# A streaming encoder step on one core: the last phase takes subln_g into A's weights, moves two transposes and the cached upper halves, and shortens a root

## The chip, the core and the metric

The kernel runs on one core of a Trainium2 chip. The metric is the time of one execution on the device in microseconds (us). Five engines work side by side, each through its own instructions in a fixed order: TensorE (PE in the profile; its weight loads are PEld), VectorE (DVE), ScalarE (ACT), GpSimd (POOL) and SyncE (SP), which here issues all transfers between the memories. SBUF and PSUM are the on-chip memories of 128 partitions; matrix products land in PSUM, in banks of 512 float32 per partition.

## What is computed

One layer for 2048 frames of a new stream (16 tiles of 128 rows) and for 8 running streams with 16 new frames each (one more tile of 128 rows, "the sample tile", with caches of 512 past keys and values for each stream). Two attention branches, A (four heads of 128 values, a difference of two softmaxes) and B (eight heads, stick-breaking), end in a merge:

```python
oa = rms_norm(oa, subln_g) * (1.0 - lam_init)
ya = (oa.reshape(b, s, WIDTH_A) * jax.nn.silu(za)) @ w_branch_a
yb = (ob.reshape(b, s, WIDTH_B) * jax.nn.silu(zb)) @ w_branch_b
return (jax.nn.sigmoid(ga) * ya + jax.nn.sigmoid(gb) * yb) @ w_out
```

The result, times a gate, is added to x, and a last rms_norm with final_g gives y. subln_g has 128 values, the same for each head of A.

## The kernel before

Every product that must be exact is made of float16 halves: `split` writes an upper half `hi = f16(src * s)` with a power of two `s`, and VectorE the lower half `lo = src * s - hi`; a product is then three float16 products (hi hi, hi lo, lo hi). The upper half is made by ScalarE, by GpSimd or by VectorE, by the last argument of `split` (lines 266 to 274). `scales` finds `s` from a sum of squares, six tiny VectorE instructions with the reduction; `rsqrt` finds a root from a guess by bits and three Newton steps, 15 instructions on VectorE for one column (lines 227 to 244).

First come the projections and the attention of the 16 prompt tiles, with o, z (the inputs of silu) and g (ga and gb) parked in DRAM. The last phase, which is what nearly all of the change touches, takes one tile after the other:

- `inputs(t)` (from line 1113) loads o, z and g, multiplies A's half of o with the root of its squares and with g8 (subln_g times 0.8, line 1127: one instruction for each head), makes silu (sigmoid of z on ScalarE into a PSUM bank of the tag "mm", o * z on GpSimd at 1132, times the sigmoid on VectorE at 1133), the sigmoids of g, then u16, the float16 halves of u, and turns them over to uT with 16 transposes on TensorE (`transposed`, 1106 to 1111, into banks of the tag "s", copied by ScalarE).
- `branches(st)` makes four products of 12 matmuls (1235, two columns halves of 512 for A and for B, banks "mm"), scales each by iu and g on VectorE (1237) and adds A and B on GpSimd (1239). After the last, `finish` cuts y into y16 and turns it to yT.
- `output(t, st)` makes two products of 24 matmuls with w_out (1274), the gate (1278), the sum with x on GpSimd (1282), the root of its squares, the last scaling (1287) and the store (1288).

There are two banks "mm" (branches and sigmoids), three "s" (transposes and the sample's scores), two "o" and one "t". Of o2, z2, u16, y16 and yT there is one buffer each, of uT two, of g2 four (two tiles).

Round n of the loop emits the branches of tile n, `inputs` of tile n + 2 and the output of tile n - 1; the first two `inputs` run before, during the end of the attention, with the cuts of the branch weights (`early_work`). Beside it run the pieces of the sample lane (`sample`, in the first 13 rounds): for each of 8 units, four loads of cached keys and four of cached values (512 KB each), each cut into halves (lines 715 and 751; the upper half on GpSimd), the keys turned over by a transposing DMA (717), the scores, the weights and 96 to 192 small matmuls (766).

The order in which the text emits work is a priority and not the final order. The framework plans the program on a simulated timeline

```python
with tile.TileContext(nc, schedule_with_timeline_sim=True) as tc:
```

and gives each engine, SP's queue among them, a fixed order: whatever the plan held to be ready, the earliest emitted first. On the chip an instruction waits for its inputs, and all behind it on its engine wait too.

Of the kernel before, what the change touches and what calls it, by code (L numbers as in the profile page):

```python
# [16 lines left out]
F32 = mybir.dt.float32  # L17
# [94 lines left out]
def layer_kernel(ctx: ExitStack, tc: tile.TileContext, a: dict):  # L112
# [132 lines left out]

    def sum_squares(src, n, dst, width=1024):

        for i in range(0, n, width):
            junk = tiny.tile([P, width], F16, tag="junk", name="junk", bufs=1)
            w = min(width, n - i)  # L250
            S.activation(out=junk[:, 0:w], in_=src[:, i : i + w], func=AF.Square,  # L251
                         accum_out=dst[:, i // width : i // width + 1])
# [26 lines left out]
    nlam = con.tile([P, 1], F32, name="nlam")  # L279
    g8 = con.tile([P, P], F32, name="g8")  # L280

# [403 lines left out]
    def sample(U, dec, qpad, cs):  # L685
# [115 lines left out]
    def norms():  # L801

        srcs = [w[:, k, :] for w in (w_ba, w_bb) for k in range(4)] + [w_out[:, k, :] for k in range(KT)]
        srcs = [(src, wsums[:, i : i + 1]) for i, src in enumerate(srcs)]
        srcs += [(caches[name][:, i * 8 : i * 8 + 8, h * P : (h + 1) * P], csums[:, cache_column(name, h), i : i + 1])
                 for name in caches for h in range(4) for i in range(4)]

        def one(src, dst):
            st = wst.tile([P, 2, 4, P], F32, tag="wst", name="wst").rearrange("p k j n -> p (k j n)")
            load(out=st if len(src.shape) == 2 else st.rearrange("p (j n) -> p j n", n=P), in_=src)  # L810
            sum_squares(st, 1024, dst)

        return [lambda src=src, dst=dst: one(src, dst) for src, dst in srcs]

# [60 lines left out]
    with tc.tile_pool(name="p0", bufs=1) as p0:  # L875
# [223 lines left out]
    def cut(dst, src, k, j, s, n, pool, tag, bufs):  # L1099

        st = pool.tile([P, 2, 512], F32, tag=tag, name="wst2", bufs=bufs)
        cols = slice(j * 512, (j + 1) * 512)
        load(out=st, in_=src[:, k : k + 2, cols])
        split(dst[:, 0, k : k + 2, cols], dst[:, 1, k : k + 2, cols], st, s[:, 0:1], S if n % 2 else G)

# [7 lines left out]
    def inputs(t):  # L1113
# [10 lines left out]
        r = L["orms"][:, 4 * t : 4 * t + 4] if t < NT else rsqrt(osums[:, NT, :], 4, P, tiny, "rA")  # L1124
        for h in range(4):
            c = slice(h * P, (h + 1) * P)
            V.scalar_tensor_tensor(out=o[:, c], in0=o[:, c], scalar=r[:, h : h + 1], in1=g8, op0=ALU.mult, op1=ALU.mult)  # L1127
        for n in range(2):
            c = slice(n * 512, (n + 1) * 512)
            sg = bank("mm")  # L1130
            act(out=sg, in_=z[:, c], func=AF.Sigmoid)
            G.tensor_tensor(out=o[:, c], in0=o[:, c], in1=z[:, c], op=ALU.mult)
            V.tensor_tensor(out=o[:, c], in0=o[:, c], in1=sg, op=ALU.mult)  # L1133
        for g in gs:
# [11 lines left out]
        return dict(u=uT, iu=iu, g=gs)  # L1146

# [4 lines left out]
    def early_work():  # L1152
# [13 lines left out]
        made = [lambda k=k, j=j, br=br: cut(L["wb"][:, br, :, :, :], (w_ba, w_bb)[br], k, j, L["s"][0], br + k, stage, "wst2", 1)  # L1166
                for br in range(2) for k in (0, 2) for j in range(2)]
# [35 lines left out]
    with ExitStack() as c2:  # L1203
# [9 lines left out]
        for n, (k, j) in enumerate((k, j) for j in range(2) for k in range(0, KT, 2)):  # L1213
            cut(wo, w_out, k, j, s_o, n, s2, "x", 2)
        gate = res.tile([P, D], F32, name="gate")
# [10 lines left out]
        def branches(st):  # L1226
# [16 lines left out]
            def finish():  # L1243
# [8 lines left out]
                yT = s2.tile([P, 16, P], F16, tag="yT", name="yT", bufs=1)  # L1252
                for half in range(2):
                    transposed(y16, yT, half)
                iy = unit.tile([P, 1], F32, tag="iy", name="iy")
                V.tensor_tensor(out=iy, in0=sy[:, 1:2], in1=s_o[:, 1:2], op=ALU.mult)
                st["y"], st["iy"] = yT, iy

            return [(2.6, lambda j=j, br=br: half(j, br)) for j in range(2) for br in range(2)]

        def output(t, st):
            box = {}

            def half(j):
# [18 lines left out]
                if j == 1:  # L1283
                    acc = tiny.tile([P, 1], F32, tag="facc", name="facc")
                    sum_squares(x, D, acc)
                    r = rsqrt(acc, 1, D, tiny, "rF")
                    V.scalar_tensor_tensor(out=x, in0=x, scalar=r, in1=fg, op0=ALU.mult, op1=ALU.mult)
# [60 lines left out]
```

## Time and profile before

| | us |
|---|---|
| median of 3 runs | 2494.43 (2491.0 to 2498.75) |
| the profiled execution | 2503.67 |
| its span, first to last instruction | 2501.9 |

| engine | busy us | share of the span |
|---|---|---|
| TensorE | 2162.8 | 86% |
| VectorE | 1807.2 | 72% |
| ScalarE | 1602.2 | 64% |
| GpSimd | 833.8 | 33% |

The first matmul of a branch product starts at 1922.8 us. The sample lane's last cut lies at 2365 us, the last output matmul ends near 2489 us, and the span ends at 2501.9 us. A busy share is a mean over stages with different limits, so the prediction reads the last phase in stretches. Where rows of waits are shown, an engine stood idle before the instruction on the left until the one on the right had ended.

### The profile page before, as it was taken

The numbers are of one execution on the slowest core, as the hardware profiler recorded it, in microseconds if no ns is written. First come the engines' busy times: TensorE is split into PE (matmuls) and PEld (weight loads), VectorE is DVE, ScalarE is ACT, GpSimd is POOL, SyncE is SP. The second block draws the span as 40 slices with busy tenths as digits, with TensorE's granted clock in tenths as the row PEclk, the third lists the DMA queues.
The fourth block names the chain that finished last, engine by engine and source line by source line (L and its number), as shares of the span: only waits on it lengthen the run. The fifth ranks groups of instructions, "written<-read, shape, count | busy, mean of one in ns | idle before, by whom it ended". The sixth has DMA issues, their size and how long they took to land.

```text
span 2501.9 us, 45310 instructions
## 1 busy us (share of the span) xinstructions
PE 2162.8 (86%) x16366; PEld 1263.7 (51%) x16366; DVE 1807.2 (72%) x3769; ACT 1602.2 (64%) x3200; POOL 833.8 (33%) x671
## 2 busy tenths in 40 slices
PE   4779898889989988899989889999975789888887
PEld 2445465545655555556555555555543344444443
DVE  4868657876665788667668866656787888787855
ACT  4658667876766778666677866656775545454442
POOL 1822023352101335321124532102353465443422
PEclk7989999999999999999999999999986889899999
DMA  8779778996777899777688976656678998997521
GB/s 304 270 184 215 183 185 202 207 209 158 187 204 170 202 206 223 169 158 184 165 201 190 217 178 168 168 134 141 146 170 214 270 232 238 225 237 209 155 97 52
DMA packets 890994, 477.07 MB, mean 191 GB/s; under 512 B 540074, under 2 KB 842330, under 8 KB 890256
## 3 DMA queue, kind: packets, MB, share of 16 engines
q1 hardware_dynamic: 890768, 474.17, 76.2%
q8 instruction: 128, 2.10, 0.4%
q14 instruction: 98, 0.80, 0.1%
HBM read 272.94 MB, written 73.44 MB: 138 GB/s over the span
## 4 chain that ended last, share of the span: by engine, by line
PE 40%; DMA 19%; DVE 16%; ACT 9%; issue 8%; POOL 4%; SPq 3%; DVEq 0%; POOLq 0%; ACTq 0%
PE ps_mm L409 16%; PE ps_t L476 9%; DMA hg<-hT_d 5%; DMA wt<-sc_n 4%; DMA wst<-in_w_in_dram 3%; DVE sc_n L588 3%; PE ps_s L611 2%; PE ps_mm L1235 2%; PE ps_s L612 2%; ACT junk L251 2%; ACT sc_p L121 2%; PE ps_o L1274 2%; DVE sc_n L545 1%; ACT ps_s L121 1%; DVE o L1127 1%
## 5 line engine op out<-in xcount | busy, mean ns | idle before, releaser
L409 PE MATMUL ps_mm<-wpair,hg 128*128 128x512 f16 x3120 | 790.1, 388 | 58.5 <-DMA hg<-hT_d 54.8
L594 POOL TENSOR_TENSOR sc_p<-sc_p,sc_n 128x127 f32<-128x127 f32 (+7 forms) x192 | 313.5, 1637 | 808.5 <-DVE sc_n L588 790.8
L409 PEld LDWEIGHTS <-hg 128*128 128x128 f16 x3120 | 279.2, 99 | 330.7 <-DMA hg<-hT_d 67.2
L476 PE MATMUL ps_t<-gw,hg 128*128 128x256 f16 (+1 forms) x2856 | 393.8, 292 | 2.5 <-DVE qst L504 1.7
L476 PEld LDWEIGHTS <-hg 128*128 128x128 f16 x2856 | 278.7, 99 | 96.3 <-DVE qst L504 2.5
L588 DVE TENSOR_TENSOR_SCAN sc_n<-ps_s,sc_n,zero_t 128x512 f32<-128x512 f32 x192 | 245.6, 1279 | 69.2 <-ACT ps_s L121 64.5
L611 PE MATMUL ps_s<-k,qst 128*128 128x512 f16 (+3 forms) x640 | 228.1, 358 | 52.4 <-DVE sc_n L588 41.3
L545 DVE TENSOR_TENSOR sc_n<-sc_p,sc_n 128x128 f16<-128x128 f32 (+7 forms) x192 | 234.5, 1227 | 36.8 <-ACT sc_n L544 36.2
L121 ACT ACTIVATE sc_p<-ps_s,usc 128x512 f32<-128x512 f32 (+3 forms) x320 | 204.8, 640 | 48.7 <-PE ps_s L612 24.0
L612 PE MATMUL ps_s<-k,qst 128*128 128x512 f16 (+3 forms) x640 | 227.6, 358 | 0.0
L1235 PE MATMUL ps_mm<-wb,uT 128*128 128x512 f16 x816 | 200.0, 398 | 21.4 <-DVE o L1133 13.0
L121 ACT ACTIVATE ps_s<-ps_s,usc 128x512 f32<-128x512 f32 (+3 forms) x328 | 199.8, 609 | 0.0
L1274 PE MATMUL ps_o<-wo,yT 128*128 128x512 f16 x816 | 193.8, 392 | 6.7 <-POOL wo L271 4.8
L663 PE MATMUL ps_o<-v,wt 128*128 128x128 f16 x1088 | 162.3, 228 | 42.4 <-DMA wt<-sc_n 42.4
L544 ACT CAST sc_n<-sc_p 128x128 f16<-128x128 f32 (+7 forms) x192 | 154.8, 813 | 44.3 <-POOL sc_p L594 43.4
L442 POOL TENSOR_TENSOR rot<-pr,rope 128x256 f32<-128x256 f32 x68 | 60.5, 890 | 358.7 <-ACT pr L423 314.6
L251 ACT ACTIVATE junk<-wst 128x1024 f16<-128x1024 f32 x124 | 131.4, 1059 | 71.8 <-DMA wst<-in_w_in_dram 23.9
L530 DVE TENSOR_SCALAR_CACHE_REDUCE sc_p<-ps_s,usc 128x512 f32<-128x512 f32 (+3 forms) x160 | 106.5, 666 | 77.7 <-PE ps_s L612 48.3
L663 PEld LDWEIGHTS <-wt 128*128 128x128 f16 x1088 | 106.1, 103 | 95.3 <-DMA wt<-sc_n 49.8
L664 PE MATMUL ps_o<-v,wt 128*128 128x64 f16 x1088 | 150.6, 200 | 0.0
L530 DVE TENSOR_SCALAR_CACHE_REDUCE sc_n<-ps_s,usc 128x512 f32<-128x512 f32 (+3 forms) x160 | 106.5, 666 | 49.3 <-PE ps_s L615 31.3
L1235 PEld LDWEIGHTS <-uT 128*128 128x128 f16 x816 | 81.1, 102 | 119.2 <-issue 39.7
(295 smaller groups left out, 4343.9 us busy)
## 6 DMA issues: line engine op xcount, KB each, us to landing
hg<-hT_d SPq DMA_DIRECT2D x130, 512.0 KB, 4.7
wst<-in_w_in_dram SPq DMA_DIRECT2D x112, 256.0 KB, 4.0
g<-g_d SPq DMA_DIRECT2D x34, 512.0 KB, 6.4
wst<-in_w_in_dram SPq DMA_DIRECT2D x32, 512.0 KB, 4.4
out_dram<-pr SPq DMA_DIRECT2D x204, 64.0 KB, 2.3
g_d<-gt SPq DMA_DIRECT2D x102, 128.0 KB, 3.6
wide<-in_w_ada_dram SPq DMA_DIRECT2D x12, 1024.0 KB, 10.8
z_d<-pr SPq DMA_DIRECT2D x136, 64.0 KB, 2.4
```

Of the source, the lines that this page charges most:

```text
L121: i = S.activation(**kw)
L409: T.matmul(box["p"], box["h"][:, hi, k, :], U["w"][k][:, wi, :], start=(n == 0), stop=(n == 3 * KT - 1))
L476: T.matmul(box["g"][:, 0:gw], box["h"][:, hi, k, :], U["wg"][k // per][:, k % per, wi, :], start=(j == 0), stop=(j == 3 * KT - 1))
L530: V.tensor_scalar(out=dst[:, lo : lo + n], in0=p[:, 0:n], scalar1=sc_pos, scalar2=None, op0=ALU.mult, op1=ALU.max, accum_out=job["mx"][:, ...
L545: V.tensor_tensor(out=lo, in0=src, in1=hi, op=ALU.subtract)
L588: V.tensor_tensor_scan(out=dst[:, lo : lo + n][:, ::-1], data0=src[:, 0:n][:, ::-1], data1=zero_t[:, 0:1].to_broadcast([P, n]), initial=fi ...
L594: G.tensor_tensor(out=p[:, 0:m], in0=p[:, 0:m], in1=n[:, 1 : m + 1], op=ALU.mult)
L611: T.matmul(p[:, 0:n], qst[:, c, :], kk[:, c, 0:n], start=True, stop=False)
L612: T.matmul(p[:, 0:n], qst[:, 2 + c, :], kk[:, c, 0:n], start=False, stop=not diag)
L663: T.matmul(po[:, c * P : (c + 1) * P], wt[:, wj, :], vt[:, c, :, :], start=first, stop=False)
L1235: T.matmul(pb, st["u"][:, ui * 8 + br * 4 + k, :], wb[:, br, wi, k, c], start=(n == 0), stop=(n == 11))
L1274: T.matmul(po, st["y"][:, yi * 8 + k, :], wo[:, wi, k, c], start=(n == 0), stop=(n == 3 * KT - 1))
```

## The change

- g8 becomes a column of 128 values, one for each row of A's weights within a head, and goes into the scale with which w_branch_a is cut (`sa`); the squares that give the scale's power of two are taken of the rows times g8 (`scale=` of `sum_squares`).
- `inputs` no longer multiplies o by root and g8 ahead. o * z comes first; A's half then takes the sigmoid and the root in one instruction for each head, which reads the sigmoid from PSUM. B's half is as it was.
- u16 is turned over a round later: `turned` for tile n + 1 stands in round n behind its second branch product, and `inputs` of tile n + 2 behind that, ahead of the third.
- y16 is turned over by `turned_y` at the end of the round, behind the output product of the tile before.
- The upper halves of the cached keys and values are made by ScalarE.
- The last root (`rsqrt_one`) is 10 instructions in place of 15.

```diff
+    def rsqrt_one(sums, width, pool, name):
+        c = tiny.tile([P, 4], F32, tag="r1", name="r1")
+        q, t, w = c[:, 0:1], c[:, 1:2], c[:, 2:3]
+        i = c[:, 3:4].bitcast(I32)
...
+        V.scalar_tensor_tensor(out=t, in0=y, scalar=y, in1=q, op0=ALU.mult, op1=ALU.mult)
+        V.tensor_scalar(out=w, in0=t, scalar1=0.375, scalar2=-1.25, op0=ALU.mult, op1=ALU.add)
+        V.tensor_scalar(out=w, in0=w, scalar1=t, scalar2=1.875, op0=ALU.mult, op1=ALU.add)
+        V.tensor_tensor(out=y, in0=y, in1=w, op=ALU.mult)
+        V.scalar_tensor_tensor(out=t, in0=y, scalar=y, in1=q, op0=ALU.mult, op1=ALU.mult)
+        V.tensor_scalar(out=w, in0=t, scalar1=-0.5, scalar2=1.5, op0=ALU.mult, op1=ALU.add)
+        V.tensor_tensor(out=y, in0=y, in1=w, op=ALU.mult)
...
-            split(k16[:, :, 0, :], k16[:, :, 1, :], kc.rearrange("p j (c d) -> p (j c) d", c=2), sk, G)
+            split(k16[:, :, 0, :], k16[:, :, 1, :], kc.rearrange("p j (c d) -> p (j c) d", c=2), sk, S)
...
-            split(v16[:, :, 0, :], v16[:, :, 1, :], vc, sv, G)
+            split(v16[:, :, 0, :], v16[:, :, 1, :], vc, sv, S)
...
-        load(out=g8, in_=a["subln_g"][0:1, :].to_broadcast([P, P]))
+        load(out=g8, in_=a["subln_g"].rearrange("o p -> p o"))
...
-        for h in range(4):
-            c = slice(h * P, (h + 1) * P)
-            V.scalar_tensor_tensor(out=o[:, c], in0=o[:, c], scalar=r[:, h : h + 1], in1=g8, op0=ALU.mult, op1=ALU.mult)
         for n in range(2):
             c = slice(n * 512, (n + 1) * 512)
             sg = bank("mm")
             act(out=sg, in_=z[:, c], func=AF.Sigmoid)
             G.tensor_tensor(out=o[:, c], in0=o[:, c], in1=z[:, c], op=ALU.mult)
-            V.tensor_tensor(out=o[:, c], in0=o[:, c], in1=sg, op=ALU.mult)
+            if n == 1:
+                V.tensor_tensor(out=o[:, c], in0=o[:, c], in1=sg, op=ALU.mult)
+            else:
+                for h in range(4):
+                    c = slice(h * P, (h + 1) * P)
+                    V.scalar_tensor_tensor(out=o[:, c], in0=sg[:, c], scalar=r[:, h : h + 1], in1=o[:, c], op0=ALU.mult, op1=ALU.mult)
...
-        uT = inp.tile([P, 16, P], F16, tag="uT", name="uT", bufs=2)
-        for half in range(2):
-            transposed(u16, uT, half)
...
+    def turned(st):
+        st["u"] = uT = L["inp"].tile([P, 16, P], F16, tag="uT", name="uT", bufs=2)
+        for half in range(2):
+            transposed(st["u16"], uT, half)
...
+        sa = con.tile([P, 1], F32, name="sa")
+        V.tensor_tensor(out=sa, in0=L["s"][0][:, 0:1], in1=g8, op=ALU.mult)
...
+            if t == tiles[0]:
+                turned(states[t])
...
+        def turned_y(st):
+            st["y"] = yT = s2.tile([P, 16, P], F16, tag="yT", name="yT", bufs=1)
+            for half in range(2):
+                transposed(st["y16"], yT, half)
...
-                    r = rsqrt(acc, 1, D, tiny, "rF")
+                    r = rsqrt_one(acc, D, tiny, "rF")
...
                 work += branches(states[tiles[n]])
+            if n + 1 <= NT:
+                work.insert(2, (0.9, lambda n=n: turned(states[tiles[n + 1]])))
             if n + 2 <= NT:
-                work.append((0.1, lambda n=n: states.update({tiles[n + 2]: inputs(tiles[n + 2])})))
+                work.insert(3, (0.1, lambda n=n: states.update({tiles[n + 2]: inputs(tiles[n + 2])})))
             if n > 0:
                 work += output(tiles[n - 1], states.pop(tiles[n - 1]))
+            if n <= NT:
+                work.append((0.9, lambda n=n: turned_y(states[tiles[n]])))
             interleave(work, aside(n))
```

More of the change, by code (lines that the diff above doesn't have):

```diff
@@ L244, in rsqrt, with sum_squares @@
         return y
-    def sum_squares(src, n, dst, width=1024):
+    def rsqrt_one(sums, width, pool, name):
+        c = tiny.tile([P, 4], F32, tag="r1", name="r1")
+        q, t, w = c[:, 0:1], c[:, 1:2], c[:, 2:3]
+        i = c[:, 3:4].bitcast(I32)
+        V.tensor_scalar(out=q, in0=sums, scalar1=1.0 / width, scalar2=EPS, op0=ALU.mult, op1=ALU.add)
+        V.tensor_scalar(out=i, in0=q.bitcast(I32), scalar1=1, scalar2=None, op0=ALU.logical_shift_right)
+        y = pool.tile([P, 1], I32, tag=name, name=name)
+        V.tensor_scalar(out=y, in0=i, scalar1=-1.0, scalar2=1597463007.0, op0=ALU.mult, op1=ALU.add)
+        y = y.bitcast(F32)
+        V.scalar_tensor_tensor(out=t, in0=y, scalar=y, in1=q, op0=ALU.mult, op1=ALU.mult)
[5 more added lines that the diff above has]
+        V.tensor_tensor(out=y, in0=y, in1=w, op=ALU.mult)
+        return y
+    def sum_squares(src, n, dst, width=1024, scale=1.0):
         for i in range(0, n, width):
@@ L279, in layer_kernel @@
     nlam = con.tile([P, 1], F32, name="nlam")
-    g8 = con.tile([P, P], F32, name="g8")
+    g8 = con.tile([P, 1], F32, name="g8")
     nh2 = con.tile([P, 1], F32, name="nh2")
@@ L1213, in layer_kernel @@
         for n, (k, j) in enumerate((k, j) for j in range(2) for k in range(0, KT, 2)):
-            cut(wo, w_out, k, j, s_o, n, s2, "x", 2)
+            cut(wo, w_out, k, j, s_o[:, 0:1], n, s2, "x", 2)
         gate = res.tile([P, D], F32, name="gate")
@@ L1251, in finish @@
                     split(y16[:, 0, c], y16[:, 1, c], st["g"][j][:, 1, :], sy[:, 0:1], S)
-                yT = s2.tile([P, 16, P], F16, tag="yT", name="yT", bufs=1)
-                for half in range(2):
-                    transposed(y16, yT, half)
                 iy = unit.tile([P, 1], F32, tag="iy", name="iy")
                 V.tensor_tensor(out=iy, in0=sy[:, 1:2], in1=s_o[:, 1:2], op=ALU.mult)
-                st["y"], st["iy"] = yT, iy
+                st["y16"], st["iy"] = y16, iy
             return [(2.6, lambda j=j, br=br: half(j, br)) for j in range(2) for br in range(2)]
+        def turned_y(st):
+            st["y"] = yT = s2.tile([P, 16, P], F16, tag="yT", name="yT", bufs=1)
+            for half in range(2):
+                transposed(st["y16"], yT, half)
         def output(t, st):
```

18 lines of the change are left out of this document (9 added, 9 removed).

## The prediction

> **What bounds the kernel now.** I first cut the span into stretches. All parts of the change but two small ones work behind 1922 us, where tiles of 128 rows are turned into the output: first beside the sample lane (stretch of 415 us), then alone (90 us), then a tail (37 us). Columns: busy time and instructions of each engine, the granted TensorE clock, the DMA share.
>
> ```profile
> 1960.00:2375.00 415.00, 355.47 (x2993) 184.56 (x2992) 351.56 (x705) 204.56 (x342) 202.84 (x141) 0.91 0.82 220
> 2375.00:2465.00 90.00, 83.60 (x454) 40.05 (x452) 54.31 (x156) 39.39 (x60) 23.84 (x19) 0.98 0.26 88
> 2465.00:2502.00 37.00, 23.24 (x113) 10.11 (x110) 14.24 (x46) 7.43 (x12) 6.32 (x5) 0.90 0.13 50
> ```
>
> In the lane stretch TensorE is busy for 86% and idle for 59.5 us; VectorE is close behind with 85%. ScalarE and GpSimd are half empty. So TensorE sets the pace, and what can be won is its idle time and what the clock loses (0.91 beside 0.98 once the lane is done). Next I asked what ended TensorE's idle time (us in total, times, longest): the first eight rows are the lane stretch, the last two what follows it.
>
> ```profile
> PE ps_s L1110 <- ACT y L269: 16.5, 14, 3.9
> PE ps_t L766 <- DMA dwt<-dsc: 8.8, 5, 2.4
> PE ps_mm L1235 <- DVE o L1133: 5.8, 3, 4.7
> PE ps_t L766 <- ACT ot L769: 5.0, 4, 2.6
> PE ps_s L1110 <- DVE y L274: 4.2, 6, 1.4
> PE ps_s L1110 <- ACT yT L1111: 3.9, 1, 3.9
> PE ps_mm L1235 <- DVE g L1237: 2.7, 1, 2.7
> PE ps_mm L1235 <- DVE rs_t L242: 2.2, 1, 2.2
> ...
> PE ps_s L1110 <- ACT yT L1111: 2.8, 2, 1.5
> PE ps_mm L1235 <- DVE g L1237: 2.8, 1, 2.8
> ```
>
> The largest item is y: its transposes (L1110) reach the head of TensorE's queue before its two halves are cut; 16.5 + 4.2 = 20.7 us. Then I looked at where these transposes stand in TensorE's order.
>
> ```profile
> 2117.81 7.72 PE L1274 MATMUL ps_o<-wo,yT 128*128 128x512 f16 x35
> 2125.37 3.62 PE L1235 MATMUL ps_mm<-wb,uT 128*128 128x512 f16 x16
> 2132.89 2.07 PE L1110 MATMUL ps_s<-id,y 128*128 128x128 f16 x16 [3.91 <-ACT y L269]
> ...
> 2436.74 0.61 PE L1110 MATMUL ps_s<-id,u 128*128 128x128 f16 x8 [1.33 <-ACT yT L1111]
> ```
>
> The text of the kernel emits y's transposes ahead of the output product, yet they run behind its 35 matmuls and even behind 16 of the next tile. The order on an engine comes from a planner that puts what it holds to be ready first. So the stall means that the chain to y is later on the chip than the planner thinks, and not that the transposes were emitted too early.
>
> **The change, part by part.** VectorE first: rows of the lane stretch (busy us, mean ns), then duration ns min/median/max of two of them over the whole run.
>
> ```profile
> L274 DVE SCALAR_TENSOR_TENSOR v16c<-dc,s_c,v16c 128x1024 f16<-128x1024 f32 x32 | 49.1, 1533 | 7.9 <-POOL v16c L271 7.9
> L274 DVE SCALAR_TENSOR_TENSOR k16c<-dc,s_c,k16c 128x1024 f16<-128x1024 f32 x28 | 47.9, 1712 | 18.2 <-POOL k16c L271 18.1
> L1127 DVE SCALAR_TENSOR_TENSOR o<-o,orms,g 128x128 f32<-128x128 f32 x48 | 30.6, 690 | 6.1 <-DMA o<-o_d 6.1
> L1133 DVE TENSOR_TENSOR o<-o,ps_mm 128x512 f32<-128x512 f32 x25 | 16.6, 676 | 4.8 <-ACT ps_mm L121 4.7
> L240 DVE TENSOR_TENSOR rs_t<-rF 128x1 f32<-128x1 f32 x33 | 14.4, 436 | 0.9
> L243 DVE TENSOR_TENSOR rF<-rF,rs_t 128x1 f32<-128x1 f32 x33 | 9.6, 291 | 0.9
> L241 DVE TENSOR_TENSOR rs_t<-rs_t,rs_q 128x1 f32<-128x1 f32 x33 | 7.6, 231 | 1.0
> L242 DVE TENSOR_SCALAR rs_t<-rs_t 128x1 f32<-128x1 f32 x33 | 5.0, 150 | 0.8
> ...
> L1127 DVE SCALAR_TENSOR_TENSOR o<-o,orms,g x64: 335/342/1445, 1861.2 to 2412.9; 128x128 f32<-128x128 f32 x64
> L274 DVE SCALAR_TENSOR_TENSOR k16c<-dc,s_c,k16c x32: 1266/1286/2276, 1928.1 to 2315.2; 128x1024 f16<-128x1024 f32 x32
> ```
>
> *Root with the sigmoid.* The four L1127 of a tile go, and the A half of L1133 becomes four instructions of 128 columns that read the sigmoid from PSUM. Removed: 30.6 us and half of L1133, 8.3 us. Added: 48 instructions. No row shows this form; below is the undisturbed L1127, 0.335 us, above its present mean, 0.690 us. I take 0.345, since L1133, which reads one operand from PSUM like the new form, has its mean at the 676 ns of an undisturbed pass, whereas the two-SBUF-operand L1127 has twice its median. Saved: 38.9 - 16.6 = 22.3 us (with 0.690: 5.8). [...]
>
> *Shorter root.* 15 instructions become 10, five of the twelve in the loop go: 5/12 of 36.6 = 15.2 us.
>
> *Cached upper halves.* 64 passes move from GpSimd to ScalarE. With GpSimd emptier, the lower halves come nearer their 1.286: the excess is 97.0 - 60 x 1.286 = 19.8 us; GpSimd keeps more than half of its work, so I take half, 10 us (ends 0 and 19.8).
>
> Together VectorE loses some 47 of 351.6 us and falls from 85% to 73%. That is worth time only where TensorE waits for it: the chain to y runs through six tiny VectorE instructions, and PSUM banks are held until L1237 has run. Now the price on ScalarE:
>
> ```profile
> L269 ACT ACTIVATE u<-o,su 128x1024 f16<-128x1024 f32 x13 | 14.8, 1141 | 10.5 <-DVE su L224 10.5
> ...
> L271 POOL TENSOR_SCALAR v16c<-dc,s_c 128x1024 f16<-128x1024 f32 x31 | 42.6, 1375 | 10.0 <-issue 8.0 <-PE ps_t L766 1.4 <-POOL g L1239 0.6
> L271 POOL TENSOR_SCALAR k16c<-dc,s_c 128x1024 f16<-128x1024 f32 x28 | 35.5, 1267 | 64.3 <-DMA dc<-in_cache_b_k_dram 21.1 <-DMA dc<-in_cache_a_k_dram 15.7 <-issue 10.5
> ```
>
> A pass of this shape costs ScalarE 1.141 us (the row of u): 64 x 1.141 = 73 us at most, 204.6 to 278 of 415 us, 67%: not the bound. GpSimd loses 42.6 + 35.5 = 78 us. But 21.1 + 15.7 = 36.8 us in which GpSimd now stands and waits for a cache load move along, and behind the wait on ScalarE are queued the squares and cuts of u and y and the copies of the transposes; on GpSimd it was three sums a tile. SP's queue stays in the same bind: the transposing DMA of the keys (L717) waits for VectorE's half, which waits for ScalarE's. I price this by a third of 36.8 in front of the chain to y, half of that hidden by the output product: 6 us. Ends: 0, and 36.8 - 16.5 = 20.3 (all of it, less what TensorE already waits for y today).
>
> *u a product later.* Today u's second half finds no free PSUM bank until yT is copied: 3.9 + 2.8 = 6.7 us. In the middle of the branches u was cut long ago, and y's transposes are elsewhere; I take 6 (ends 0 and 6.7). The bank of u's transposes is then shared with the lane's scores, which the copies release as now.
>
> *y a product later.* By the order shown, the new place is where the transposes already run: nothing by itself. Cover: the output product of 48 matmuls; were it gone, the 20.7 us would grow. But the chain before it changes: less queueing on VectorE, its last sum on GpSimd no longer behind a cache pass. I take 8 of 20.7 (ends 0 and 20.7; what ScalarE adds is the 6 above).
>
> *Banks held behind VectorE.* 2.7 + 2.2 + 2.8 = 7.7 us of waits of the branches for L1237, queued behind L1127's wait for its load or a root; I take 4 (ends 0, 7.7). The 5.8 us for L1133 stay: the sigmoid still takes a branch bank.
>
> *inputs() earlier in the order.* Its four loads of a tile go to SP's queue half a product earlier in the text, but each waits for its buffer: o for the cut of the tile before, g for the cut of y. No gain counted; a loss stands below as a rival. *subln_g in the weights*: one [128,1] product, four cuts and four squares with another scale, one load of 128 elements in place of a broadcast, all far ahead of 1850 us or beside the weights: 0 (ends -3, +3: the weights' cuts at 1900 to 1925 wait for their loads).
>
> *Tail.* The last tile's root is on the path:
>
> ```profile
> 2492.33 1.28 DVE L1287 SCALAR_TENSOR_TENSOR x<-x,rF,fg 128x1024 f32<-128x1024 f32 x1
> 2493.53 0.14 DVE L232 TENSOR_SCALAR rs_q<-facc 128x1 f32<-128x1 f32 x1
> ...
> 2496.20 0.16 DVE L243 TENSOR_TENSOR rF<-rF,rs_t 128x1 f32<-128x1 f32 x1
> 2496.45 1.28 DVE L1287 SCALAR_TENSOR_TENSOR x<-x,rF,fg 128x1024 f32<-128x1024 f32 x1
> ```
>
> From 2493.53 to 2496.45 are 15 instructions in 2.92 us, 0.195 each; five less are 0.97 us. The root of the tile before ends on the same engine at 2492.33 and holds it up: 0.97 again. -1.9 us.
>
> *Clock.* Idle 14% goes with a clock of 0.91, idle 7% with 0.98: a point each. The terms of the lane, -6 - 8 - 4 + 6 = -12, are 2.9% of 415 us; 0.029/0.91 of 355 us is 11 us. The lane's small matmuls may also share in the 0.91, so I take 6 (ends 0 and 11). [...]
>
> Sum: -6 - 8 - 4 + 6 - 6 - 1.9 = -19.9 us. The profiled execution took 2503.67 us (span 2501.9), 9.24 above the median of 2494.43; so 2483.8 for it, and 2474.5 for the median.
>
> **The rivals.**
> *ScalarE's queue becomes the wait (slower).* A late cache load now holds up everything that TensorE waits for. For it: 36.8 us of such waits, and y's cut is the largest wait already. Against it: GpSimd, which loses them, stands in the same chain. Price: +20.3, nothing won on y or clock: -6 - 4 + 20.3 - 1.9 = +8.4, 2503. It decides from 20 us of new waits on.
> *The sigmoids take the branches' banks (slower).* inputs() now stands ahead of the last two branch products, both kinds share two banks, and z is loaded before o: a sigmoid may hold a bank while o is still loading. The trace has it once, 4.7 us in the row of L1133. At one such wait in each of the 11 lane tiles: 52 - 20 = +32, 2526; in half of them +6, 2500. It decides from four tiles on for no gain. Against it: the planner sees the banks.
> *It doesn't do what it says.* The order stays, VectorE was no cause: only the tail and u's bank, -7.9, 2486.5, or the tail alone, 2492.5.
>
> **How the numbers follow.** Forecast 0.58; ScalarE's queue 0.14; banks 0.11; nothing but tail and bank 0.17. 0.3% (7.5 us) is about what a measurement of this kernel can tell from no change; the three runs shown spread by that much. Faster: 0.58 and a quarter of the last case, 0.62; same: the rest of that and a little of the slower ones, 0.15; slower 0.23. The forecast's own range is 2455 to 2487. With every favourable end (6.7 + 20.7 + 7.7 + 11 + 1.9 = 48) it would be 2446; the upper end takes in ScalarE's 2503 and the banks in half the tiles. 2450 to 2508.
>
> **What would show it.** Right: waits of y's transposes for ScalarE or VectorE well under 20.7 us in the lane, none of L1110 for yT; VectorE near 300 us in the lane stretch; the granted clock over 0.93; the new 128-column form at 0.35 us; ten root instructions at the end. Wrong: ScalarE waiting for dc loads by 30 us or more with y's transposes behind it; L1235 waiting for the sigmoid's product in many tiles; a lane stretch as long as now with VectorE much emptier, which would say that VectorE was never what TensorE waited for.

## The result, and the profile after

The changed kernel takes 2481.93 us (median of 6, 2475.7 to 2485.09) beside 2498.5 us for the kernel before on the same chip: a ratio of 0.9943, 95% interval 0.9924 to 0.9962. Measured once more beside other kernels it is 0.9929. So 14 to 18 us are gained where the prediction said 19.9. The number came out; the working, as the experiments show, did not, so the number was in good part luck.

The stretches of the profiled execution of the changed kernel (columns as in the prediction: busy time and instructions of PE, PEld, DVE, ACT and POOL, granted clock, DMA share, GB/s):

```profile
1960.00:2375.00 415.00, 359.96 (x3008) 190.29 (x3007) 298.50 (x637) 257.56 (x393) 117.64 (x81) 0.90 0.78 209
2375.00:2465.00 90.00, 85.60 (x451) 40.95 (x449) 46.38 (x116) 35.91 (x54) 22.95 (x18) 0.98 0.19 65
```

VectorE fell from 351.6 to 298.5 us, much as forecast. TensorE hardly profited: idle for 55.0 us instead of 59.5, at a clock of 0.90 instead of 0.91. (The window is fixed, and the changed kernel enters it further on in its work; the whole last phase is compared below.) VectorE's groups in the lane, with the new 128-column form at the forecast price (0.342 us) and the lower halves of the cache nearer their undisturbed 1.286:

```profile
L293 DVE SCALAR_TENSOR_TENSOR v16c<-dc,s_c,v16c 128x1024 f16<-128x1024 f32 x30 | 43.0, 1435 | 5.6 <-ACT v16c L288 5.5
L293 DVE SCALAR_TENSOR_TENSOR k16c<-dc,s_c,k16c 128x1024 f16<-128x1024 f32 x26 | 35.9, 1379 | 24.3 <-ACT k16c L288 24.3
...
L1154 DVE SCALAR_TENSOR_TENSOR o<-ps_mm,orms,o 128x128 f32<-128x128 f32 x44 | 12.4, 342 | 9.4 <-ACT ps_mm L121 7.2 <-issue 2.2
```

TensorE's waits in the lane (us in total, times, longest):

```profile
PE ps_s L1129 <- DVE dsc L607: 21.9, 2, 12.6
PE ps_s L1129 <- ACT y L288: 10.3, 9, 4.7
PE ps_s L1129 <- ACT yT L1130: 7.4, 3, 3.3
PE ps_s L1129 <- DVE y L293: 5.1, 4, 1.9
```

The rows give 15.4 us to the waits for y (20.7 before), those for yT's copy have grown from 3.9 us to 7.4, and a new one of 21.9 us has come. It is the transposes' wait for a bank that the lane's scores hold. Here is the longer of its two cases, in order of time, all engines, other instructions left out:

```profile
1998.53 5.34 PE L1263 MATMUL ps_mm<-wb,uT 128*128 128x512 f16 x24
...
2004.10 2.94 DVE L293 SCALAR_TENSOR_TENSOR y<-g,sy,y 128x512 f16<-128x512 f32 x2
2005.40 2.19 SPq L1142 DMA_DIRECT2D g<-g_d  x2
...
2007.45 1.15 ACT L288 ACTIVATE k16c<-dc,s_c 128x1024 f16<-128x1024 f32 x1 [2.77 <-DMA dc<-in_cache_a_k_dram]
...
2009.92 1.06 ACT L121 ACTIVATE g<-g 128x1024 f32<-128x1024 f32 x1 [0.28 <-DMA g<-g_d]
...
2012.37 1.06 ACT L121 ACTIVATE g<-g 128x1024 f32<-128x1024 f32 x1 [1.39 <-DMA g<-g_d]
...
2014.40 0.67 ACT L121 ACTIVATE ps_s<-ps_s,dsf 128x512 f32<-128x512 f32 x1
...
2015.10 1.28 DVE L607 TENSOR_TENSOR_SCAN dsc<-ps_s,dsc,zero_t 128x512 f32<-128x512 f32 x1 [0.73 <-ACT ps_s L121]
...
2016.43 1.87 PE L1129 MATMUL ps_s<-id,y 128*128 128x128 f16 x16 [12.56 <-DVE dsc L607]
```

TensorE ends its branch product at 2003.87. y is cut by 2007.04, so 3.2 us of the stall are y. The other 9.4 are a chain through the loads that the change moved ahead: SP can issue the loads of g for the tile after next (2005.40) only as y's cut sets their buffers free (SP waits for that cut twice from 1998 to 2018, 2.5 us in all); ScalarE stands for a cache load and then for those of g; and the evacuation of the scores is queued behind both sigmoids of g, so that the scan on VectorE, which frees the bank, ends at 2016.38. In the other case (9.3 us) y was cut before TensorE came to it, and the same chain is all of the stall. Counted by time and not by what ended them, TensorE's waits ahead of y's transposes are 20.3 us up to the end of y's cut and 18.8 us behind it, where before has 21.1 and 0.3: y itself is waited for about as long as before.

The tail, VectorE and then GpSimd: ten root instructions between 2466.66 and 2468.71, 2.14 us up to the scaling instead of 2.92. From TensorE's last matmul to the end of the span it is 10.61 us instead of 12.96.

```profile
2464.43 1.00 DVE L262 TENSOR_TENSOR rF<-rF,r 128x1 f32<-128x1 f32 x1
...
2466.66 0.15 DVE L251 TENSOR_SCALAR r<-facc 128x1 f32<-128x1 f32 x1
...
2468.55 0.16 DVE L262 TENSOR_TENSOR rF<-rF,r 128x1 f32<-128x1 f32 x1
2468.80 1.28 DVE L1317 SCALAR_TENSOR_TENSOR x<-x,rF,fg 128x1024 f32<-128x1024 f32 x1
```

```profile
2464.15 1.26 POOL L1312 TENSOR_TENSOR x<-m,x 128x512 f32<-128x512 f32 x1 [2.42 <-DVE m L1308]
```

Last, where the last phase begins: the row of the last matmul of the attention (duration in ns, first and last start), of before and then of after.

```profile
L664 PE MATMUL ps_o<-v,wt x1088: 191/193/262, 334.9 to 1915.3; 128*128 128x64 f16 x182
```

```profile
L683 PE MATMUL ps_o<-v,wt x1088: 190/193/262, 322.9 to 1887.8; 128*128 128x64 f16 x182
```

From there to the end of the span before takes 586.6 us and after 586.0. Both in one row each, before and then after:

```profile
1915.30:2501.90 586.60, 489.79 (x3664) 246.35 (x3662) 450.42 (x958) 269.61 (x439) 252.30 (x177) 0.91 0.71 193
```

```profile
1887.80:2473.80 586.00, 487.96 (x3665) 248.94 (x3662) 399.76 (x857) 336.92 (x503) 162.36 (x113) 0.89 0.71 193
```

VectorE has 51 us less to do, and TensorE is idle for 98.0 us instead of 96.8. The last phase, of which nearly the whole change is made, has gained nothing in these two executions; the time was won ahead of it. (The two executions are 28 us apart, the medians 17.)

### The profile page after: what moved, and what is told of

Its sections match the earlier page's. It is cut to its first block, busy times and chain, and to the rows that moved or that the text cites. A ratio compares the mean times of both kernels' runs of the same rounds, so it can differ in the third digit from the quotient of the medians.

```text
span 2473.8 us, 45248 instructions
## 1 busy us (share of the span) xinstructions
PE 2149.5 (87%) x16366; PEld 1262.2 (51%) x16366; DVE 1759.2 (71%) x3668; ACT 1668.6 (67%) x3264; POOL 743.0 (30%) x607
## 4 chain that ended last, share of the span: by engine, by line
PE 29%; DMA 11%; DVE 11%; ACT 7%; issue 5%; SPq 2%; POOL 2%; DVEq 0%; ACTq 0%; POOLq 0%
PE ps_mm L428 8%; PE ps_t L495 6%; PE ps_o L1304 4%; PE ps_mm L1263 3%; DVE sc_n L607 3%; DMA hg<-hT_d 2%; DMA wt<-sc_n 2%; DMA dc<-in_cache_a_k_dram 2%; PE ps_s L630 1%; DVE sc_n L564 1%; PE ps_s L631 1%; DMA g<-g_d 1%; DMA dc<-in_cache_b_k_dram 1%; ACT junk L270 1%; ACT sc_p L121 1%
## 5 line engine op out<-in xcount | busy, mean ns | idle before, releaser
L613 POOL TENSOR_TENSOR sc_p<-sc_p,sc_n 128x127 f32<-128x127 f32 (+7 forms) x192 | 308.4, 1610 | 792.5 <-DVE sc_n L607 783.2
L1263 PE MATMUL ps_mm<-wb,uT 128*128 128x512 f16 x816 | 192.9, 392 | 16.4 <-DVE o L1154 10.2
L461 POOL TENSOR_TENSOR rot<-pr,rope 128x256 f32<-128x256 f32 x68 | 66.4, 976 | 368.8 <-ACT pr L442 331.2
L607 DVE TENSOR_TENSOR_SCAN sc_n<-ps_s,zero_t 128x128 f32<-128x128 f32 (+3 forms) x128 | 104.3, 815 | 51.2 <-ACT ps_s L121 45.3
L1263 PEld LDWEIGHTS <-uT 128*128 128x128 f16 x816 | 80.2, 100 | 116.0 <-issue 20.5
```

Of the source, the lines that this page charges most:

```text
L607: V.tensor_tensor_scan(out=dst[:, lo : lo + n][:, ::-1], data0=src[:, 0:n][:, ::-1], data1=zero_t[:, 0:1].to_broadcast([P, n]), initial=fi ...
L613: G.tensor_tensor(out=p[:, 0:m], in0=p[:, 0:m], in1=n[:, 1 : m + 1], op=ALU.mult)
L1263: T.matmul(pb, st["u"][:, ui * 8 + br * 4 + k, :], wb[:, br, wi, k, c], start=(n == 0), stop=(n == 11))
```

## The experiments

Three questions: does the gain lie ahead of the last phase or in it; which parts gain and which lose; and by what mechanism. The table has every kernel that ran. "Last phase" is the time from the start of the last attention matmul to the end of the span; idle and clock are TensorE's in the stretch 1960 to 2375; "y" is what the rows of waits there give to y's transposes waiting for y's cut; the last two columns are means over the 10 to 13 tiles that have both ends in that stretch, counted from the traces: TensorE's busy time between a tile's last branch matmul and its first y transpose (the cover; matmul records overlap, as the 24 of L1263 above, which take 5.34 us together where one has a median of 0.379, and overlapping time counts once), and the time from the end of that matmul to the end of y's cut (the chain).

Three limits go with the table. Each kernel's trace is one execution, which can lie up to 16 us off the median of its kernel (u_early's has 2506.9 us beside 2491.4, and is the slowest of 12). The stretch is fixed, so it holds different parts of the work: 2703 matmuls in turns_only, 3144 in no_turns. And the framework plans each kernel anew: TensorE's order in the last phase is the same in two traces of one kernel and differs between every two kernels compared below, so the worth of a part includes the plan that came with it.

| kernel | ratio to before (95%) | last phase | idle, clock | y | cover | chain |
|---|---|---|---|---|---|---|
| before | 1 | 586.6 | 59.5, 0.91 | 20.7 | 13.9 | 19.2 |
| before_again | 0.9989 (0.9972 to 1.0005) | 587.9 | 59.0, 0.91 | 23.7 | 13.6 | 19.1 |
| after | 0.9943 (0.9924 to 0.9962) | 586.0 | 55.0, 0.90 | 15.4 | 9.9 | 11.8 |
| after_again | 0.9929 (0.9905 to 0.9953) | 589.3 | 59.2, 0.89 | 13.9 | 9.9 | 11.8 |
| weights_only | 0.9970 (0.9956 to 0.9985) | 581.7 | 60.3, 0.91 | 23.1 | 13.2 | 18.1 |
| g8_only | 0.9912 (0.9888 to 0.9935) | 575.3 | 59.6, 0.91 | 12.7 | 13.7 | 18.8 |
| weights_sig_root | 0.9861 (0.9844 to 0.9878) | 568.2 | 48.4, 0.94 | 15.1 | 12.8 | 17.3 |
| halves_only | 0.9909 (0.9894 to 0.9924) | 561.3 | 53.5, 0.96 | 8.9 | 17.0 | 20.5 |
| turns_only | 1.0102 (1.0081 to 1.0123) | 610.3 | 83.5, 0.88 | 31.7 | 10.0 | 15.1 |
| rest_only | 1.0043 (1.0029 to 1.0058) | 596.8 | 70.3, 0.90 | 16.9 | 10.4 | 12.9 |
| no_turns | 0.9767 (0.9742 to 0.9793) | 543.6 | 35.9, 0.95 | 6.0 | 14.6 | 16.7 |
| u_late | 0.9827 (0.9800 to 0.9853) | 553.9 | 41.4, 0.95 | 11.7 | 12.9 | 15.5 |
| u_early | 0.9988 (0.9970 to 1.0007) | 601.6 | 80.2, 0.88 | 22.3 | 7.5 | 12.9 |
| y_only | 0.9800 (0.9776 to 0.9824) | 552.5 | 41.9, 0.95 | 0 | 18.2 | 14.5 |

### The two kernels again, and the change cut in two

before_again and after_again are unchanged. g8_only has subln_g in the weights and the root with the sigmoid, nothing else; rest_only has all the other parts and keeps line 1127 and the broadcast of subln_g.

> The kernel before once more, unchanged: what the same program differs by from run to run. In the two traces the attention's last matmul of the values (the end of the attention) came at 1915 us before and at 1888 us after the change, although no line of the attention was changed, and what is left of the span is the same, 586.6 and 586.0 us. Theory P (the plan: the attention's order was changed by the planner through the new load of subln_g, and that is the gain): this run ends the attention within 5 us of 1915, ratio 0.998 to 1.002. Theory S (scatter: the attention differs by this much from run to run, and the median's gain lies in the last phase): the attention ends somewhere between 1888 and 1915 us, 8 us or more away from 1915.

> The changed kernel once more. Theory P: the attention ends within 5 us of 1888 again and the rest of the span is 583 to 590 us, ratio 0.992 to 0.996. Theory S: the attention ends near 1900 to 1915 us and the rest is 570 to 578 us, with the same ratio.

> Of the change only subln_g in A's weights and the root with the sigmoid; transposes, upper halves and the last root as before. The engines' order in the attention is that of the changed kernel instruction for instruction. Theory P: most of the gain is here, ratio 0.991 to 0.996, attention end near 1888 us, the rest about as long as before (580 to 590 us). Theory S: ratio 0.997 to 1.001, since only 22 us of VectorE work go, beside a TensorE that sets the pace.

> Of the change all but subln_g and the root with the sigmoid: u and y transposed later, upper halves on ScalarE, shorter last root. The order in the attention is that of the kernel before. Theory P: ratio 0.998 to 1.003, attention end near 1915 us. Theory S: ratio 0.993 to 0.996, the rest of the span 10 to 16 us shorter than 586.6 us. My prediction's own sum puts about 15 us here (transposes, banks, clock, tail) and lies with theory S.

Neither theory came out whole. The attention of before_again ends at 1905.6 us and that of after_again at 1893.1: it scatters by more than the 5 us that theory P allowed, and yet the two kernels stay 12 us apart with last phases of the same length, which theory S ruled out. g8_only has the ratio of theory P, but its attention ends at 1911.3 us in the trace and its last phase is shorter, 575.3 us. rest_only, which theory S and the prediction's own sum had faster, has a last phase 10 us longer than before.

g8_only gains more than the whole change (0.9912), rest_only loses (1.0043). So the parts on which the prediction spent its terms together cost time, and the part that it counted only through others carries the gain.

### subln_g in the weights alone

```diff
-            V.scalar_tensor_tensor(out=o[:, c], in0=o[:, c], scalar=r[:, h : h + 1], in1=g8, op0=ALU.mult, op1=ALU.mult)
+            V.scalar_tensor_tensor(out=o[:, c], in0=o[:, c], scalar=r[:, h : h + 1], in1=L["one"], op0=ALU.mult, op1=ALU.mult)
...
+        V.tensor_tensor(out=sa, in0=L["s"][0][:, 0:1], in1=g8, op=ALU.mult)
```

`L["one"]` holds ones, and the cuts of A's weights use `sa`.

> subln_g in A's weights alone; the pass with the root stays where it was, on VectorE, with ones in place of subln_g, so every instruction of the last phase has the form it had before. The order of the attention's instructions is that of the changed kernel. VectorE theory (the 22 us that the root with the sigmoid saves on VectorE are the gain): 2496 us, no change beyond 5 us; the last phase (end of the last attention product to the end of the span) 584 to 592 us. Order theory (the gain sits ahead of 1915 us, in another order of the attention): 2480 us, last phase 584 to 592 all the same.

0.9970 is 7.5 us: neither theory. The VectorE theory asked for no change beyond 5 us, the order theory for 16. TensorE's matmuls of the attention stand in one order in all kernels that load subln_g as a column (weights_only leaves it near the end, at 1859 us), and in another in the rest: the two orders part after TensorE's first 614 matmuls, at 157 us. That the new load shifts the plan of the whole program is the likely reason. The last attention matmul starts at 1897.0 us in the mean of the nine profiles with the new order (1887.8 to 1911.3) and at 1911.8 in the five with the old one (1905.6 to 1916.3). That is 15 us, though the two ranges overlap, and the timed runs of this kernel show only half of it. The root with the sigmoid is worth the rest, 0.9970 to 0.9912, 14.5 us. With it the waits for y fall, and the idle time of the whole last phase from 96.1 to 88.1 us; in the fixed stretch idle time and clock are as before. TensorE's rows of weights_only, then of g8_only:

```profile
PE ps_s L1110 <- ACT y L269: 17.8, 13, 5.6
...
PE ps_s L1110 <- DVE y L274: 5.3, 7, 1.4
```

```profile
PE ps_s L1110 <- ACT y L269: 9.7, 9, 3.9
...
PE ps_s L1110 <- DVE y L274: 3.0, 3, 2.5
```

### The upper halves alone

```diff
-            split(k16[:, :, 0, :], k16[:, :, 1, :], kc.rearrange("p j (c d) -> p (j c) d", c=2), sk, G)
+            split(k16[:, :, 0, :], k16[:, :, 1, :], kc.rearrange("p j (c d) -> p (j c) d", c=2), sk, S)
...
-            split(v16[:, :, 0, :], v16[:, :, 1, :], vc, sv, G)
+            split(v16[:, :, 0, :], v16[:, :, 1, :], vc, sv, S)
```

> Only the cached upper halves go to ScalarE. Queue theory (ScalarE standing for cache loads holds up the cuts of y and the copies of the transposes): this alone carries the loss of the three parts together, 2504 us or more, and the waits of y's transposes for ScalarE in the lane rise from 16.5 us to 25 or more. Transposes theory (the loss comes from the transposes a product later): 2496 us within 5, waits of y's transposes as before. By my prediction's own term: +6 less the easing of VectorE's lower halves, 2493 to 2500.

Both theories fall, and the price of the prediction's own term too: 0.9909, a gain of 22.7 us. The last phase of halves_only, TensorE's two rows for y, and ScalarE's two rows for the keys' loads:

```profile
1913.80:2475.10 561.30, 474.54 (x3664) 239.55 (x3661) 420.49 (x958) 334.16 (x503) 162.62 (x113) 0.94 0.76 202
```

```profile
PE ps_s L1110 <- ACT y L269: 7.9, 5, 3.0
...
PE ps_s L1110 <- DVE y L274: 1.0, 3, 0.4
```

```profile
ACT k16c L269 <- DMA dc<-in_cache_a_k_dram: 20.1, 7, 9.6
...
ACT k16c L269 <- DMA dc<-in_cache_b_k_dram: 15.8, 7, 4.5
```

ScalarE does stand 35.9 us for those loads, as the rival said, and yet y is waited for less. The chain to y is no shorter (20.5 us, 19.2 before). But TensorE's order puts 17.0 us of other work ahead of the transposes instead of 13.9, so more of the chain is covered. The clock rises with it, in the last phase 0.94 for 0.91: the same 3664 matmuls keep TensorE busy for 474.5 us instead of 489.8, and with 10 us less of idle time (86.8 for 96.8) that is the 25 us by which the last phase is shorter. Why the plan puts more work there was not tested.

### The transposes alone

The edit is the change's own, in `inputs`, `branches` and the main loop.

> Only the transposes of u and y a product later (with the loads of the tile after next moved ahead). Queue theory: no loss, 2488 to 2496 us; the 6.7 us of waits for yT's copy are gone. Transposes theory: 2503 us or more. By my prediction's own terms, -6 and a part of -8: 2485 to 2490.

1.0102, a loss of 25 us: the transposes theory's 2503 us or more came true, while the queue theory falls, and with it the prediction's own 2485 to 2490. The lane stretch of turns_only, and TensorE's waits:

```profile
1960.00:2375.00 415.00, 331.46 (x2703) 171.90 (x2703) 336.94 (x679) 194.61 (x320) 188.00 (x135) 0.88 0.81 216
```

```profile
PE ps_s L1110 <- ACT y L269: 25.5, 8, 13.1
PE ps_s L1110 <- ACT ps_mm L121: 14.6, 1, 14.6
...
PE ps_s L1110 <- ACT yT L1111: 6.7, 1, 6.7
```

The waits for yT's copy, which the prediction took as gone, are 6.7 us here, and the waits for y are longer than before the change.

### With the shorter root, and without the transposes

weights_sig_root is g8_only with the shorter root. no_turns is the changed kernel with both transposes and the loads back at their old places.

> subln_g in the weights, the root with the sigmoid, and the shorter root; halves and transposes as before. VectorE theory: the five instructions less of a tile's root help further, 2470 to 2476 us. Chain theory (VectorE is no longer what TensorE waits for): as without the shorter root but for the tail, 2476 to 2481 us.

> The changed kernel with the transposes of u and y back at their old places and the loads of the tile after next back behind the branches: subln_g in the weights, the root with the sigmoid, the halves on ScalarE and the shorter root stay. Moves theory (the moves cost what turns_only lost, some 25 us): 2452 to 2462 us, below every kernel so far. Saturation theory (halves and roots take away the same waits, and the moves cost only where these are not done): 2468 to 2482 us.

The shorter root takes the ratio from 0.9912 to 0.9861, 12.7 us and more than either theory allowed. no_turns is the fastest kernel of all: 2436.25 us beside 2495.94, and below the range that either theory gave. The halves are worth 23.5 us on this base (0.9861 to 0.9767), as much as alone. The lane stretch of no_turns, TensorE's rows for y, and ScalarE's for the keys' loads:

```profile
1960.00:2375.00 415.00, 379.13 (x3144) 193.83 (x3144) 301.90 (x692) 274.43 (x421) 131.94 (x89) 0.95 0.82 221
```

```profile
PE ps_s L1129 <- ACT y L288: 4.2, 7, 1.0
...
PE ps_s L1129 <- DVE y L293: 1.8, 6, 0.5
```

```profile
ACT k16c L288 <- DMA dc<-in_cache_b_k_dram: 22.7, 9, 5.4
ACT k16c L288 <- DMA dc<-in_cache_a_k_dram: 22.0, 9, 4.4
```

The fastest kernel has ScalarE stand 44.7 us for cache loads, more than the changed kernel (20.7 and 18.2). So such waits need not cost anything; what counts is what is queued behind them.

### The moves one by one

All three start from no_turns. u_late moves only u's transposes to the middle of the next branches; u_early moves `inputs` of the tile after next as well; y_only moves only y's transposes.

```diff
+                work.insert(2, (0.9, lambda n=n: turned(states[tiles[n + 1]])))
             if n + 2 <= NT:
-                work.append((0.1, lambda n=n: states.update({tiles[n + 2]: inputs(tiles[n + 2])})))
+                work.insert(3, (0.1, lambda n=n: states.update({tiles[n + 2]: inputs(tiles[n + 2])})))
```

u_late has the first line only, u_early all of them.

> no_turns, and of the moves only u's transposes in the middle of the next branches; the loads of the tile after next stay behind the branches. Loads theory (what costs is that these loads stand earlier in SP's queue and wait there for y's cut with the cache loads behind them; its row rose from 12.8 to 37.8 us in turns_only): within 5 us of no_turns, the waits of SP for y in the lane at 8 to 15 us. Transposes-of-u theory: 10 us or more above no_turns.

> As u_late, and the loads, squares and sigmoids of the tile after next ahead of the second pair of branch halves, as in the changed kernel; y's transposes at their old place. Loads theory: 12 us or more above u_late, SP's waits for y at 28 us or more in the lane. Transposes-of-y theory (only y_only loses): within 5 us of u_late.

> no_turns with y's transposes alone behind the output product of the tile before in the text. Loads theory: within 5 us of no_turns, since they already ran there. Transposes-of-y theory: 10 us or more above no_turns, with longer waits of the transposes or of the output product for yT. My prediction's term: up to 8 us below no_turns.

u's transposes cost 15 us (0.9767 to 0.9827), as the transposes-of-u theory had it and not within the 5 of the loads theory; moving `inputs` ahead costs 40 us more (0.9988), as the loads theory had it; y's transposes alone cost 8 (0.9800; itself uncertain by some 8), between the two theories and not the gain that the prediction's term allowed, and behind u_early they give 11 to 15 back, since u_early and y_only together are the changed kernel (0.9943, 0.9929). With u's transposes moved, y's cover falls from 14.6 to 12.9 us and y's waits rise from 6.0 to 11.7; the rest of the 15 us was not followed up. The loads theory is right on which move is dear, but not on the mechanism. SP's waits for y's cut, in no_turns, u_late and u_early:

```profile
SPq L1142 <- DVE y L293: 20.8, 13, 7.8
```

```profile
SPq L1142 <- DVE y L293: 4.8, 5, 1.9
```

```profile
SPq L1142 <- DVE y L293: 28.7, 11, 7.9
```

They rise to the 28 us that the theory named, but no_turns has 20.8 us of them and is the fastest kernel: long waits in SP's queue are no loss by themselves. What costs is what stands behind the loads. The last phase of u_late and of u_early (TensorE idle for 76.2 and 115.9 us):

```profile
1893.30:2447.30 554.00, 477.81 (x3665) 240.76 (x3662) 382.22 (x857) 334.51 (x503) 166.01 (x113) 0.93 0.76 204
```

```profile
1903.50:2505.00 601.50, 485.60 (x3664) 247.09 (x3661) 391.11 (x857) 336.80 (x503) 161.80 (x113) 0.88 0.70 188
```

TensorE's waits for the scan, first of u_late, then of u_early with the next row and its time (20 us windows, columns as above):

```profile
PE ps_s L1129 <- DVE dsc L607: 1.2, 1, 1.2
```

```profile
PE ps_s L1129 <- DVE dsc L607: 30.5, 2, 20.6
PE ps_s L1129 <- ACT y L288: 19.0, 9, 6.9
```

```profile
2020.00:2040.00 20.00, 2.30 (x22) 2.40 (x23) 14.42 (x33) 12.13 (x22) 7.06 (x5) 0.50 0.90 236
2040.00:2060.00 20.00, 20.00 (x193) 10.88 (x192) 13.58 (x26) 12.24 (x18) 6.71 (x5) 0.92 0.78 207
```

It is the stall shown for the changed kernel, 20.6 us long, from 2017.1 to 2037.7. Its first half is y, whose cut ends at 2027.23:

```profile
2026.49 0.74 DVE L293 SCALAR_TENSOR_TENSOR y<-g,sy,y 128x512 f16<-128x512 f32 x1
```

The second is the chain: sigmoids that wait for loads that wait for y's cut, and behind them the evacuations that free the transposes' bank. The row of y's waits is the other part of the price: the cover of y's transposes is 7.5 us where u_late has 12.9. In u_late 42 of the 48 matmuls of the output product (mean of the tiles) stood between branches and transposes; in u_early 8 do, and in 9 of the 11 tiles most of the product runs ahead of the second pair of branch halves, which is emitted after `inputs`. The chain itself is shorter (12.9 us, 15.5 in u_late), yet y's waits double, from 11.7 to 22.3 us. In y_only the cover grows to 18.2 us and the waits for y vanish, but u's transposes wait instead:

```profile
PE ps_s L1129 <- ACT u L288: 8.1, 5, 2.8
PE ps_s L1129 <- ACT uT L1130: 5.1, 2, 4.5
PE ps_s L1129 <- DVE u L293: 4.2, 5, 1.5
```

How much of the 40 us is the bank chain and how much the lost cover, no run separates: a kernel with another bank for the transposes was not tried. The traces give about half to each: ahead of y's transposes TensorE waits in the lane stretch 11.8 us up to the end of y's cut and 0.2 us behind it in u_late, 34.0 and 20.2 in u_early. Nor was a kernel tried that loads the column of subln_g and changes nothing else.

## Why the prediction was right, and where it was not

The sum, -19.9, and what the runs give for its parts (ratios of the ladder above on 2497 us; each step is uncertain by some 5 to 8 us):

| term | predicted | measured |
|---|---|---|
| subln_g in the weights | 0 | -7.5 |
| root with the sigmoid | only through y, banks, clock | -14.5 |
| shorter root | -1.9, and through them | -12.7 |
| upper halves on ScalarE | +6 | -23.5 (alone -22.7) |
| u a product later | -6 | +15 |
| inputs() earlier | 0 | +40 |
| y a product later | 0, and -8 for its chain | -11 to -15 behind these, +8 without them |

The measured column is a ladder from the kernel before to the changed one, so it adds to the measured change by construction, -14 to -18. That the forecast came so near is luck: the moves, for which the sum has -14, cost 40 to 44 us, while the halves, for which it has +6, gave 23.5, and the weights and the two roots, with -1.9 and a share in the other terms, gave 34.7. The weights, the halves and u lie outside the ends that the prediction gave for them; `inputs`, the largest, had no term at all.

*inputs() earlier* was the step that failed worst: "No gain counted; a loss stands below as a rival". The rival was a sigmoid of z holding a branch bank, and in the changed kernel no wait of the branch products for one is among the rows of the lane (turns_only has 9.8 us of them in four waits, before 5.8 in three). The same paragraph had the true cause in hand, "each waits for its buffer: ... g for the cut of y". It did not ask what stands behind those loads: ScalarE's sigmoids, behind these the scores' evacuations, and behind these the bank for y; nor what the move does to the output product that covered y.

*Cached upper halves*: the 1.141 us for a pass held (1.141 and 1.150 in the changed kernel), ScalarE's busy time rose as said, and the move of 36.8 us of waits took place (38.9). The price put on it was wrong in sign. The wait for a load was counted as late for all that is queued behind it, but y was waited for less; what GpSimd's passes did to VectorE was counted for the lower halves alone (10 us).

*y and u a product later*: "the new place is where the transposes already run: nothing by itself" looked at y and the output product as they stood, and not at the second pair of branch halves, which now lets the output product run ahead of it. Of y's 20.7 us the sum takes 8; by time up to y's cut they went from 21.1 to 20.3. "I take 6" for u's bank: the waits for yT went from 3.9 to 7.4 us in the lane.

*VectorE*: 298.5 us for about 305 in the lane, 51 us less for 47 over the last phase, the new form 0.342 for 0.345, the tail -2.35 for -1.9. These were right, and worth more than was said: about 27 us for the two roots, while the whole lane got -12 before the clock. *Clock*: forecast above 0.93, measured 0.90; 0.94 to 0.96 stand in weights_sig_root, halves_only and no_turns, which have none of the moves.

Of the signs of being right that it named, VectorE, the new form and the ten root instructions came true; the clock, no wait for yT (7.4 us) and, counted by time, the waits for y did not. Of the signs of being wrong, ScalarE's 38.9 us for cache loads came true without the loss that it stood for, and so did "a lane stretch as long as now with VectorE much emptier", but not what it would say: the steps to g8_only and to weights_sig_root change in their text nearly only VectorE's instructions and are both faster, so the end did hang on VectorE, unless their new plans made the gain. What the emptier VectorE and the halves won in the last phase was paid back by the moves.

## What to carry to other kernels

When a step is emitted earlier, follow each of its loads to the buffer that it must wait for, and then everything queued behind the instruction that reads the load, down to the banks; here that step cost 40 us, more than any other part of the change was worth. Read a stall by its cover: how much other work stands in the waiting engine's order ahead of the instruction that waits, since a shorter chain with less cover lost time (u_early: 12.9 us with 7.5 of cover, where u_late has 15.5 with 12.9) and a longer one with more cover won it (halves_only: 20.5 with 17.0, where before has 19.2 with 13.9). And a change of several parts whose sum comes out right should still be taken apart: without the moves this one is worth 2.3% instead of 0.6%.

## What the runs showed of the hardware

**Some VectorE instructions wait for a GpSimd pass to end.** In the tail rows above, the one-column product L262 takes 1.00 us and ends at 2465.43, where GpSimd's sum (from 2464.15, 1.26 us) ends at 2465.41; four microseconds later the same instruction takes 0.16. In the trace of before, all 23 of the L1127 that began during a GpSimd pass ended 0.14 to 0.15 us after it, with a median of 1.285 us against 0.340 for the 45 others; of L240, the root's product of one or four columns, all 17 ended within 0.02 us of it, 1.053 against 0.159 (the 12 on one column, 128 numbers, 1.107). Of the lower halves of 1024 columns, L274, the 41 that began during a pass have a median of 2.127 us, the 112 others 1.279. The new form, with one operand in PSUM, shows no such wait (0.342 during a pass, 0.343 else), nor do the root's one-input instructions of one column (L242: 0.140 for the 4 that began during a pass, 0.154 for the 50 others), but the shift of two columns, L224, does (22 of 22, 0.522 against 0.168), and so does the one-input L242 on four columns (5 of 5, 1.077 against 0.170). What makes the difference, no row shows. In the lane VectorE lost this way some 74 us before, 67 in g8_only, 43 in weights_sig_root, 48 in halves_only and 25 in no_turns (the excess over the lower quartile of the same instruction, summed over those longer than 1.3 times it that overlap a GpSimd pass). It is a likely reason for the worth of the shorter root, whose two-input products are among what waits; no run separates it.

**The granted clock after a long stall.** In the 20 us rows of u_early the granted clock is 0.50 where TensorE is busy for 2.30 us, at the end of the long stall, and 0.92 in the row after it, in which TensorE is busy throughout (20.00 us). From 2080 to 2100 it is busy throughout as well, and the clock is 1.00. Beside that row the one after the stall lost 0.08 x 20 = 1.6 us, an estimate: the stall cost more than its length. The number of long waits alone does not give the clock of the lane: halves_only, with two waits over 3 us instead of four, has 0.96 where before has 0.91, but weights_sig_root, with five, has 0.94.
